# Inverse square roots of the norms: a power of -0.5 on GpSimd and one Newton step in place of a bit trick and three steps

## The chip, the cores and the metric

The kernel runs on one core of a Trainium2 chip. The metric is the device time of one execution in microseconds (us). Durations of single instructions come from one profiled execution, which has its own time and its own span (the time from the first to the last recorded instruction).

## The reference, cut to what matters

A diffusion backbone of four layers works on 256 context tokens and 256 latent tokens of width 1024. Layers 0 and 3 mix tokens by windowed attention (16 query heads, 4 key heads), layer 1 by multi-head latent attention (16 heads), layer 2 by a recurrent unit. After each mixer comes a gated feed-forward part of width 2816 with a short convolution. Every sublayer starts with a norm over the token's 1024 features, and the attentions norm every head of queries and keys, and in layer 1 also the two low-rank vectors:

```python
def rmsnorm(x, gain):
    xf = x.astype(jnp.float32)
    y = xf * lax.rsqrt(jnp.mean(xf * xf, axis=-1, keepdims=True) + EPS)
    return (y * gain.astype(jnp.float32)).astype(x.dtype)
```

## The kernel before, in words

The residual stream X lies transposed: eight tiles of 128 features by 512 tokens, context tokens in columns 0 to 255 and latent tokens in columns 256 to 511. Matrix products are made nearly exact by splitting each operand into a rounded part (hi) and the remainder (lo) and adding three products (`mm3`, lines 227 to 229: hi with hi, lo with hi, hi with lo; which operand's part is which depends on the caller). Weights come from memory in units of up to 128 x 1024 (`load`, L207), with three buffers; `convert` rounds a unit on ScalarE (whi, L214) and subtracts on GpSimd (wlo, L218), in four pieces of 256 columns or in one. This subtraction, and some of the lo parts of the normed activations (L442), are nearly all that GpSimd does.

The place of the change is `mean_rsqrt` (L276). It takes sums of squares, one column of 128 tokens (or one head) each, scales them by 1/dim and adds EPS (rs_v, L278), and returns the inverse square root. `rsqrt` (L264) halves the number's bits and subtracts them from a constant (L268, L269), and refines this guess by three Newton steps of three instructions (L271, L272, L273). All are on VectorE, each needs the one before, and each works on 128 partitions by 2, 4, 8 or 16 columns.

The callers are these. `Norm.rsq` (2 columns): squares on ScalarE and sums on VectorE (L413, L415), TensorE adds over features (L423), mean_rsqrt, and TensorE spreads the result over 128 rows (L427); `Norm.apply` then multiplies (hn, L437) and splits into h_hi (L438) and h_lo (L442 on GpSimd, L444 on VectorE). It is called once for context and once for latent tokens between any two sublayers. `out_tail` computes the context columns of a sublayer's output first, so that the context half's norm runs while TensorE does the latent columns (their result goes to X on VectorE, L452), and then calls the latent half's norm; the next sublayer's first matmuls on context columns can run beside that one. At the end of the last layer's mixer there are latent tokens only. In windowed attention, `swa` calls mean_rsqrt once for all keys (16 columns, rk; keys are scaled at L599, turned, copied at L604 and transposed on TensorE at L609), and `q_post` once for every 128 tokens and half of the heads (8 columns; the result only scales the scores later, through rqs, L640). In latent attention, `mla` calls it for the two low-rank vectors (4 columns, L789), for the keys and the queries of the first four heads (16 columns each), and then for each 128 tokens of the next four heads, keys and queries together (8 columns; kn at L832 and L833, transposed at L837, rqs at L869). The cores of the attentions score, take the exponential, transpose the probabilities (L694 or L908) and multiply by the values (L700 or L914).

The order on each engine is made when the kernel is compiled: a scheduler simulates the engines with its own costs and, each time an engine is free, takes from the ready instructions the one that comes first in the program text. So independent instructions are put between those of a call where the simulated engine would wait. On the chip every engine then runs its list in that order, and an instruction that waits holds up those behind it. In a few places the text forces an order (`tc.issue_after`), none of them in mean_rsqrt. The tiles of mean_rsqrt come from a pool of 24 small buffers.

Of the kernel before, what the change touches and what calls it, by code (L numbers as in the profile page):

```python
# [10 lines left out]
F32 = mybir.dt.float32  # L11
# [4 lines left out]
ALU = mybir.AluOpType  # L16
# [95 lines left out]
def hybrid_kernel(ctx: ExitStack, tc: tile.TileContext, xT, cc, ccT, W, modwa, modwb, modw, colv, rowv, tabs, band, out, depth=DEPTH, dbg=None):  # L112
    nc = tc.nc
    offs, _ = unit_offsets()

    const = ctx.enter_context(tc.tile_pool(name="const", bufs=1))
# [30 lines left out]
    def small(n, name="small", dt=F32):  # L147
        return sm_p.tile([128, 32], dt, tag="small", name=name)[:, :n]
# [115 lines left out]
    def rsqrt(v, n, steps=3):  # L264
        i = small(n, "rs_i", I32)
        y = small(n, "rs_y")
        t = small(n, "rs_t")
        nc.vector.tensor_scalar(i, v.bitcast(I32), 1, None, op0=ALU.logical_shift_right)  # L268
        nc.vector.tensor_scalar(y.bitcast(I32), i, -1.0, MAGIC, op0=ALU.mult, op1=ALU.add)  # L269
        for _ in range(steps):  # L270
            nc.vector.tensor_tensor(t, y, y, op=ALU.mult)  # L271
            nc.vector.scalar_tensor_tensor(t, t, -0.5, v, op0=ALU.mult, op1=ALU.mult)  # L272
            nc.vector.scalar_tensor_tensor(y, t, 1.5, y, op0=ALU.add, op1=ALU.mult)  # L273
        return y

    def mean_rsqrt(src, n, dim):  # L276
        v = small(n, "rs_v")
        nc.vector.tensor_scalar(v, src, 1.0 / dim, EPS, op0=ALU.mult, op1=ALU.add)  # L278
        return rsqrt(v, n)

    modc = [const.tile([128, 2, 48], F32, name=f"modc{l}") for l in range(DEPTH)]
    junk = const.tile([128, D], BF16, name="junk")
    scale_c = [const.tile([128, 2, 2, 8], F32, name=f"scale{l}") for l in range(DEPTH)]
# [105 lines left out]
    class Norm:  # L389
# [28 lines left out]
        def rsq(self, sums):  # L418
            acc, sq = sums
            ps = tp_ps()  # L420
            for b in range(2):
                for z, a in enumerate((acc, sq)):
                    nc.tensor.matmul(ps[:, b:b + 1], a[:, b * 128:(b + 1) * 128], ones, start=z == 0, stop=z == 1)  # L423
            rs = mean_rsqrt(ps[:, 0:2], 2, D)
            rb = ps[:, 256:]
            for b in range(2):
                nc.tensor.matmul(rb[:, b * 128:(b + 1) * 128], rs[:, b:b + 1].to_broadcast([128, 128]), ident, start=True, stop=True)  # L427
            return rb
# [97 lines left out]
    def swa(l, i, q0, nm, nxt, first=None):  # L526
# [57 lines left out]
        for b in range(4):  # L584
# [5 lines left out]
            nc.scalar.activation(sq, kb, AF.Square)  # L590
            nc.vector.tensor_reduce(ssk[:, b * 4:(b + 1) * 4], sq.rearrange("p (h d) -> p h d", d=64), axis=AX.X, op=ALU.add)
        rk = mean_rsqrt(ssk, 16, 64)
        kh, kl = big("k_hi"), big("k_lo")

# [19 lines left out]
        def q_post(p, b, ps):  # L614
            if rqs[p] is None:
                rqs[p] = const.tile([128, 32], F32, tag=f"rqs{p}", name="rqs")
            if (p, b // 2) not in qt:
                qt[p, b // 2] = big("q").rearrange("p (b j) n -> p b j n", b=2)
            qb = qt[p, b // 2][:, b % 2]
            sq = tmp("sq")  # L620
            nc.scalar.activation(sq, ps, AF.Square)
            ss = small(8, "ssq")
            nc.vector.tensor_reduce(ss, sq.rearrange("p (h d) -> p h d", d=64), axis=AX.X, op=ALU.add)
            qr = tmp("qr")
            rotate(qr, ps, b, 8, gq, cgq, sgq)
            for z in range(2):
                hl = tmp("qhl")
                h4 = hl.rearrange("p (h s d) -> p h s d", h=4, s=2)
                q4 = qr[:, z * 256:(z + 1) * 256].rearrange("p (h d) -> p h d", h=4)
                nc.scalar.activation(h4[:, :, 0].bitcast(F32R), q4, AF.Copy)  # L630
                nc.vector.tensor_tensor(h4[:, :, 1], q4, h4[:, :, 0], op=ALU.subtract)
                pq = tp_ps()
                for j in range(4):
                    nc.tensor.transpose(pq[:, j * 128:(j + 1) * 128], hl[:, j * 128:(j + 1) * 128], ident)
                if z == 0:
                    nc.scalar.activation(qb[:, z], pq, AF.Copy)
                else:
                    nc.vector.tensor_copy(qb[:, z], pq)
            rq = mean_rsqrt(ss, 8, 64)
            nc.vector.tensor_scalar(rqs[p][:, b * 8:(b + 1) * 8], rq, 0.125, None, op0=ALU.mult)  # L640
# [694 lines left out]
```

## Time and profile before

| | |
|---|---|
| median of three runs | 2244.1 us (2243.03 to 2250.57) |
| the profiled execution | 2239.54 us, span 2237.8 us |
| busy in the span: TensorE, VectorE, ScalarE, GpSimd | 2120.5, 1572.0, 1033.3, 1046.0 us |
| mean granted clock of TensorE | 0.985 of full speed |

The engines are named PE (TensorE's matmuls), PEld (its weight loads), DVE (VectorE), ACT (ScalarE), POOL (GpSimd) and SP (the queue that issues the loads from memory). L273 is line 273 of the kernel. A busy share is an average over the whole span, so which wait ends last is read stretch by stretch. A name such as wlo<-raw,whi says which tile is written and which are read.

### The profile page before, as it was taken

Reading aid. Unit: us, or ns where it says so; the run is one execution under the profiler, and the core shown is the slowest. Engines: PE = TensorE matmul, PEld = TensorE weight load, DVE = VectorE, ACT = ScalarE, POOL = GpSimd, SP = SyncE. Lnnn points to the kernel's source line nnn. Section 1 sums busy time; section 2 is a strip of 40 time slices with the busy share of each in tenths; the row PEclk is TensorE's granted clock in tenths of the full one; section 3 lists DMA queues with packets and bytes.
Section 4 is the critical chain, followed back from the end, with each engine's and each line's share of the span. In section 5 each row is a group of like instructions: output and inputs, shape, how many; then the busy total and the mean of one; then the engine's idle time right before and its main releaser. Section 6 shows DMA issues by size and latency. Waiting matters only on the chain.

```text
span 2237.8 us, 32872 instructions
## 1 busy us (share of the span) xinstructions
PE 2120.5 (95%) x12084; PEld 1762.9 (79%) x12084; DVE 1572.0 (70%) x3342; ACT 1033.3 (46%) x1850; POOL 1046.0 (47%) x760
## 2 busy tenths in 40 slices
PE   6989999999999999999999998899999999898999
PEld 5666788888878666888888786688888887678999
DVE  4677779777776887687879689847864456785333
ACT  4467653332346775532323366634332234675544
POOL 3231155444544113444554456664544444526887
PEclk9999999999999999999999999999999999999999
DMA  8534136554532001155556422234655552313665
GB/s 300 195 123 133 39 131 193 170 173 164 174 101 68 21 29 57 60 194 175 175 179 189 140 67 81 78 93 136 194 185 167 164 168 74 104 38 107 187 181 158
DMA packets 83888, 300.14 MB, mean 134 GB/s; under 512 B 11152, under 2 KB 12816, under 8 KB 81296
## 3 DMA queue, kind: packets, MB, share of 16 engines
q1 hardware_dynamic: 83728, 298.05, 41.4%
q8 instruction: 95, 1.56, 0.3%
q14 instruction: 65, 0.53, 0.1%
HBM read 296.97 MB, written 1.05 MB: 133 GB/s over the span
## 4 chain that ended last, share of the span: by engine, by line
PE 76%; DVE 16%; ACT 4%; DMA 2%; issue 1%; POOL 1%; SPq 0%; ACTq 0%; DVEq 0%
PE fl L228 9%; PE fl L229 8%; PE fl L227 8%; PE mm L227 7%; PE mm L229 7%; PE mm L228 7%; PE mo L228 4%; PE mo L227 4%; PE mo L229 4%; PE tp L227 3%; PE tp L229 2%; PE tp L228 2%; PE mo L700 2%; PE mm L887 2%; PE tp L694 2%
## 5 line engine op out<-in xcount | busy, mean ns | idle before, releaser
L218 POOL TENSOR_TENSOR wlo<-raw,whi 128x256 fp32r<-128x256 f32 (+3 forms) x709 | 1011.4, 1448 | 1121.6 <-ACT whi L214 1086.0
L214 ACT ACTIVATE whi<-raw 128x1024 fp32r<-128x1024 f32 (+3 forms) x367 | 382.6, 1043 | 478.0 <-PE tp L228 187.8
L376 DVE SCALAR_TENSOR_TENSOR junk<-mw,cbc 128x1024 bf16<-128x1024 f32 x256 | 457.6, 1788 | 24.3 <-DMA mw<-in_modw_dram 14.7
L227 PE MATMUL fl<-h_hi,whi 128*128 128x512 f32 (+1 forms) x832 | 296.8, 358 | 3.3 <-DVE lam L961 1.7
L228 PE MATMUL fl<-h_lo,whi 128*128 128x512 f32 (+1 forms) x832 | 297.3, 358 | 0.2 <-POOL h_lo L442 0.2
L229 PE MATMUL fl<-h_hi,wlo 128*128 128x512 f32 (+1 forms) x832 | 297.2, 358 | 0.1
L228 PE MATMUL mm<-h_lo,whi 128*128 128x512 f32 (+1 forms) x768 | 269.8, 352 | 2.3 <-DVE h_lo L444 1.5
L227 PE MATMUL mm<-h_hi,whi 128*128 128x512 f32 (+1 forms) x768 | 270.6, 352 | 1.3 <-ACT h_hi L438 1.1
L229 PE MATMUL mm<-h_hi,wlo 128*128 128x512 f32 (+1 forms) x768 | 269.3, 351 | 0.0
L1112 DVE SCALAR_TENSOR_TENSOR conv<-mm,colt,conv 128x510 f32<-128x510 f32 (+1 forms) x88 | 59.8, 679 | 191.7 <-ACT conv L1110 191.7
L1116 ACT ACTIVATE conv<-conv 128x512 f32<-128x512 f32 (+1 forms) x88 | 51.0, 580 | 288.9 <-DVE conv L1114 288.9
L227 PEld LDWEIGHTS fl<-h_hi,whi 128*128 128x128 f32 x832 | 157.7, 190 | 26.2 <-DVE xc L1006 1.9
L228 PEld LDWEIGHTS fl<-h_lo,whi 128*128 128x128 f32 x832 | 158.2, 190 | 23.0 <-POOL h_lo L442 0.6
L229 PEld LDWEIGHTS fl<-h_hi,wlo 128*128 128x128 f32 x832 | 158.1, 190 | 22.9 <-POOL wlo L218 0.5
L227 PE MATMUL mo<-g_hi,whi 128*128 128x256 f32 (+1 forms) x488 | 164.8, 338 | 9.4 <-DVE x L452 6.3
L228 PE MATMUL mo<-g_lo,whi 128*128 128x256 f32 (+1 forms) x488 | 164.0, 336 | 0.4 <-DVE g_lo L262 0.4
L228 PEld LDWEIGHTS mm<-h_lo,whi 128*128 128x128 f32 x768 | 146.4, 191 | 22.8 <-DVE h_lo L444 2.3
L227 PEld LDWEIGHTS mm<-h_hi,whi 128*128 128x128 f32 x768 | 147.0, 191 | 21.0 <-ACT h_hi L438 1.9
L229 PE MATMUL mo<-g_hi,wlo 128*128 128x256 f32 (+1 forms) x488 | 163.5, 335 | 0.0
L229 PEld LDWEIGHTS mm<-h_hi,wlo 128*128 128x128 f32 x768 | 146.3, 191 | 18.6
L452 DVE SCALAR_TENSOR_TENSOR x<-mo,modc,x 128x256 f32<-128x256 f32 x212 | 95.4, 477 | 85.9 <-PE mo L229 85.6
L227 PEld LDWEIGHTS mo<-g_hi,whi 128*128 128x128 f32 x488 | 92.4, 190 | 21.9 <-DVE x L452 6.7
(313 smaller groups left out, 4376.0 us busy)
## 6 DMA issues: line engine op xcount, KB each, us to landing
raw<-in_W_dram SPq DMA_DIRECT2D x352, 512.0 KB, 3.6
mw<-in_modw_dram SPq DMA_DIRECT2D x144, 512.0 KB, 4.2
mw<-in_modwa_dram SPq DMA_DIRECT2D x8, 1024.0 KB, 16.2
mw<-in_modwb_dram SPq DMA_DIRECT2D x16, 512.0 KB, 4.7
mw<-in_modwb_dram SPq DMA_DIRECT2D x8, 1024.0 KB, 9.2
cbc<-in_cc_dram SPq DMA_DIRECT2D x3, 1024.0 KB, 5.8
raw<-in_W_dram SPq DMA_DIRECT2D x8, 384.0 KB, 3.0
x<-in_xT_dram SPq DMA_DIRECT2D x8, 256.0 KB, 3.7
```

What stands on the lines that cost most here:

```text
L214: nc.scalar.activation(hi, raw, AF.Copy)
L218: nc.gpsimd.tensor_tensor(lo[:, cs], raw[:, cs], f32(hi[:, cs]), op=ALU.subtract)
L227: nc.tensor.matmul(ps, ah, bh, start=start and i == 0, stop=False, **kw)
L228: nc.tensor.matmul(ps, ah, bl, start=False, stop=False, **kw)
L229: op = nc.tensor.matmul(ps, al, bh, start=False, stop=stop and i == n - 1, **kw)
L376: nc.vector.scalar_tensor_tensor(junk, raw, 1.0, cbc[:, s], op0=ALU.mult, op1=ALU.mult, accum_out=modc[l][:, s, m:m + 1])
L452: nc.vector.scalar_tensor_tensor(X[m][:, half], ps[:, half], modc[l][:, s, part + m:part + m + 1], X[m][:, half], op0=ALU.mult, op1=ALU.add)
L694: nc.tensor.transpose(pp[:, c:c + 128], P[z][:, (2 * kp + kk) * 128:(2 * kp + kk + 1) * 128], ident)
L700: nc.tensor.matmul(po[r], v[0][:, kb, p * 128 + 64 * z:p * 128 + 64 * z + 64], pt[:, kp, (kk * 2 + z) * 128:(kk * 2 + z + 1) * 128], start ...
L887: nc.tensor.matmul(ps[:, c], d["q"][:96, 2 * hp + z, bc], d["k"][:96, 2 * hp + z, :nk], start=True, stop=True)
L1112: op = nc.vector.scalar_tensor_tensor(y3[:, :, 1:], g3[:, :, :255], cw[:, l, 0, f:f + 1], y3[:, :, 1:], op0=ALU.mult, op1=ALU.add)
L1116: nc.scalar.activation(y[:, t0:], y[:, t0:], AF.Silu)
```

## The change

`mean_rsqrt` no longer calls `rsqrt`. It hands v to GpSimd, which raises it element by element to the power in a constant tile mhalf (-0.5), and VectorE does one Newton step on the result. mhalf is filled once at the start.

```diff
     def mean_rsqrt(src, n, dim):
         v = small(n, "rs_v")
         nc.vector.tensor_scalar(v, src, 1.0 / dim, EPS, op0=ALU.mult, op1=ALU.add)
-        return rsqrt(v, n)
-
+        y = small(n, "rs_y")
+        t = small(n, "rs_t")
+        nc.gpsimd.tensor_tensor(y, v, mhalf[:, :n], op=ALU.pow)
+        nc.vector.tensor_tensor(t, y, y, op=ALU.mult)
+        nc.vector.scalar_tensor_tensor(t, t, -0.5, v, op0=ALU.mult, op1=ALU.mult)
+        nc.vector.scalar_tensor_tensor(y, t, 1.5, y, op0=ALU.add, op1=ALU.mult)
+        return y
+
+    mhalf = const.tile([128, 32], F32, name='mhalf')
+    nc.gpsimd.memset(mhalf, -0.5)
```

## Rows read from the trace of the kernel before

**Rows 1.** The page: busy time by engine; the chain that ended last, by engine.
```profile
PE 2120.5 (95%) x12084; PEld 1762.9 (79%) x12084; DVE 1572.0 (70%) x3342; ACT 1033.3 (46%) x1850; POOL 1046.0 (47%) x760
...
PE 76%; DVE 16%; ACT 4%; DMA 2%; issue 1%; POOL 1%; SPq 0%; ACTq 0%; DVEq 0%
```

**Rows 2.** Stretch, its length; PE, PEld, DVE, ACT, POOL busy (instructions); clock, DMA share, GB/s.
```profile
270.00:303.00 33.00, 29.94 (x233) 27.98 (x233) 26.70 (x69) 16.66 (x35) 14.75 (x20) 1.00 0.20 65
...
724.00:860.00 136.00, 123.90 (x814) 89.94 (x814) 112.14 (x412) 96.19 (x237) 22.61 (x34) 0.99 0.11 32
...
1900.00:1925.00 25.00, 20.77 (x85) 16.64 (x85) 13.79 (x30) 11.83 (x23) 17.27 (x24) 0.86 0.38 107
...
2025.00:2045.00 20.00, 13.91 (x93) 13.24 (x92) 13.89 (x37) 9.40 (x19) 13.10 (x18) 0.80 0.35 106
```

**Rows 3.** TensorE's waits: waiting line, what ended the wait, us, times, longest.
```profile
PE tp L427 <- DVE rs_y L273: 13.5, 11, 3.4
...
PE tp L609 <- ACT P L604: 6.7, 2, 4.2
...
PE tp L837 <- DVE rqs L869: 5.8, 2, 3.7
PE tp L837 <- DVE kn L833: 4.4, 2, 2.3
```

**Rows 4.** Groups by line, VectorE: busy us, mean ns of one, idle time before.
```profile
L273 DVE SCALAR_TENSOR_TENSOR rs_y<-rs_t,rs_y 128x8 f32<-128x8 f32 (+3 forms) x135 | 36.2, 268 | 2.4
L271 DVE TENSOR_TENSOR rs_t<-rs_y 128x8 f32<-128x8 f32 (+3 forms) x135 | 33.2, 247 | 2.6
L272 DVE SCALAR_TENSOR_TENSOR rs_t<-rs_t,rs_v 128x8 f32<-128x8 f32 (+3 forms) x135 | 31.5, 233 | 2.2
...
L269 DVE TENSOR_SCALAR rs_y<-rs_i 128x8 int32<-128x8 int32 (+3 forms) x45 | 14.7, 327 | 1.2
...
L268 DVE TENSOR_SCALAR rs_i<-rs_v 128x8 int32<-128x8 int32 (+3 forms) x45 | 11.5, 255 | 0.9
```

**Rows 5.** Tile rs_y: duration ns (min/median/max), first and last start, forms.
```profile
L269 DVE TENSOR_SCALAR rs_y<-rs_i x45: 153/172/736, 14.2 to 2036.3; 128x8 int32<-128x8 int32 x24, 128x2 int32<-128x2 int32 x15, 128x16 int32<-128x16 int32 x4, 128x4 int32<-128x4 int32 x2
```

**Rows 6.** Chain that ended last, two calls of mean_rsqrt: start us, us, what.
```profile
279.34 0.18 DVE rs_i L268
...
284.36 0.08 DVE rs_y L273
...
1910.97 0.19 DVE rs_i L268
...
1911.39 0.69 DVE rs_t L271
...
1916.24 0.66 DVE rs_t L272
...
1916.92 0.19 DVE rs_y L273
```

**Rows 7.** The same chain: a handover from ScalarE to GpSimd to TensorE.
```profile
300.48 0.07 issue
300.55 0.75 POOL h_lo L442
301.30 0.04 issue
```

**Rows 8.** GpSimd's groups by shape: busy us, mean ns of one, idle before.
```profile
L218 POOL TENSOR_TENSOR wlo<-raw,whi 128x1024 fp32r<-128x1024 f32 x248 | 641.8, 2589 | 532.9 <-ACT whi L214 529.3 <-PE mo L229 3.5
L218 POOL TENSOR_TENSOR wlo<-raw,whi 128x256 fp32r<-128x256 f32 x440 | 357.4, 844 | 569.2 <-ACT whi L214 538.9 <-issue 12.5 <-PE mo L700 6.3
...
L218 POOL TENSOR_TENSOR wlo<-raw,whi 128x128 fp32r<-128x128 f32 x12 | 5.3, 471 | 5.1 <-ACT whi L214 5.1
```

**Rows 9.** GpSimd in order of time, beside two calls of mean_rsqrt.
```profile
279.42 3.07 POOL L218 TENSOR_TENSOR wlo<-raw,whi 128x256 fp32r<-128x256 f32 x4 [8.40 <-ACT whi L214]
...
1911.30 5.56 POOL L218 TENSOR_TENSOR wlo<-raw,whi 128x256 fp32r<-128x256 f32 x8 [2.90 <-ACT whi L214]
```

## The prediction

> **What bounds the kernel now.** First the page's busy shares and its chain that ended last: TensorE is busy for 2120.5 of 2237.8 us and 76% of the chain is TensorE, 16% VectorE, 1% GpSimd [rows 1]. So no change to VectorE can give more than the 117 us in which TensorE stands idle, and a VectorE instruction counts only where TensorE waits behind it. Then the busy time by stretch shows where that idle time lies: at the seams between sublayers and in the attention stages. The seam at 270 to 303 us leaves TensorE idle for 33.00 - 29.94 = 3.1 us, multi-head latent attention (724 to 860) for 12.1, the first 25 us of layer 3 for 4.2, its last norm (2025 to 2045) for 6.1 [rows 2]. Last TensorE's waits: the broadcast of the inverse root (L427) waited 13.5 us in 11 places for the final Newton step L273, the longest time 3.4; key transposes L609 waited 6.7 in two places and L837 4.4 in two, both a few instructions behind an inverse root [rows 3].
>
> **What is removed.** mean_rsqrt runs 45 times: 24 calls on 8 columns, 15 on 2, 4 on 16, 2 on 4 [rows 5]. Each is L278 and then eleven dependent VectorE instructions, L268, L269 and three rounds of L271 to L273. L268, L269 and two of three rounds go, eight instructions a call. In busy time that is 11.5 + 14.7 + 2/3 x (33.2 + 31.5 + 36.2) = 93.5 us, 2.1 us a call [rows 4]. It isn't one price. L269 takes 172 ns at the median and up to 736 ns [rows 5]: in the call at 1910 us L268 takes 0.19, L269 as much, the eight steps after it 0.66 to 0.69 each, and the last one 0.19 again [rows 6]; GpSimd's wlo subtractions start at 1911.30 and last 5.56 us [rows 9]. So a step costs about 0.2 us with GpSimd quiet and 0.69 beside wlo; eight cost 1.6 or up to 5.5 us.
>
> **What is added.** One hop: VectorE hands v to GpSimd, GpSimd does the power, VectorE takes y. Handovers have rows: ScalarE to GpSimd 0.07 us, GpSimd to TensorE 0.04 [rows 7]; I take 0.1 for both. No row has a power on GpSimd. From below: its subtractions take 471 ns at 128 columns and 844 at 256 [rows 8], which is 2.9 ns a column and 0.1 us for none, so 0.1 us if a power costs no more than a subtraction. From above nothing bounds a routine of another kind; the longest GpSimd instruction on record is 2.59 us [rows 8], and I keep that as the upper end of what rows show. I take 0.5 us, the subtraction at 128 columns, the narrowest on record, though it has eight or more times the elements. So the hop is 0.6 us. GpSimd's queue is in order: where wlo pieces are running (0.77 each at 279.42: 3.07 for four [rows 9]) the power waits for about half of one, so 1.0. Behind it in that queue are the next weight unit's wlo pieces, which start up to 0.5 us later; their matmuls come some microseconds afterwards at the seams, so I price that at nothing, and at 0.5 us a seam if that cover is gone. VectorE's three remaining steps wait for the power, and anything that the scheduler put behind them waits too. The memset of mhalf falls into the first 2 us and costs nothing (GpSimd is idle there until the weights come); the DMA queues gain and lose nothing.
>
> **What each place gives**, in the profiled execution's own 2239.5 us (span 2237.8):
> (a) Seams after sublayers, five alike (279/293 us, and at 652, 916, 1291, 1875). The length of a call is read from the chain of waits, from the start of L268 to the end of the last L273 (the two ends of one stand in rows 6, the others are read alike). The context call at 279 takes 5.1 us, 279.34 to 284.44 [rows 6], 1.5 of it other VectorE work put between. After: 1.0 hop, 2.0 for three steps (the wlo pieces that slowed the removed steps now meet these), about 1 between: 4.0, so 1.1 less. The latent call at 293, 4.0 us, becomes 0.6 + 1.0 + 0.8 = 2.4, so 1.6 less. Together 2.7 us of VectorE path against 3.1 of TensorE idle [rows 2], part of which has other causes (PSUM taken by L452): half comes through, 1.5 each, 7.5.
> (b) The pair at 1505 and the lone call at 2035, where TensorE waits up to 3.4 us with nothing to cover it [rows 3]. 6.1 us becomes 4.0, 3.1 becomes 2.0: 3.1 together.
> (c) The three 16-column calls whose consumers are the key transposes (64, 704, 1910 us): 4.3, 4.2 and 6.1 us (1910.97 to 1917.11 [rows 6]) become 1.0 + 2.0 = 3.0: 1.3, 1.2, 3.1, within TensorE's waits there (6.7 for the two L609, 2.3 the longest for L837 [rows 3]): 5.6.
> (d) The 12 query calls in window attention and the 13 others in latent attention. 1.6 removed, 0.6 to 1.0 added: 0.6 to 1.0 of VectorE time each, some 20 us over 25 calls, but most stand beside core work. TensorE waits 10.2 us for L837 in four places [rows 3], and about a third of that is such a call: 4, and 2 for window attention: 6.
> (e) The two calls before 17 us: nothing, since TensorE there waits next for weights from memory.
> Sum 22.2. I take 2 off for powers that delay VectorE's other instructions behind them: 20 us, 2239.5 to 2219.5. The median of the runs shown, 2244.1, lies 4.6 above the profiled execution, so on that scale 2224. What I count at nothing: the mean granted clock is 0.86 and 0.80 in two of these stretches [rows 2], between the levels of 1.2 and 2.4 GHz, where TensorE had waited up to 4.2 and 3.4 us [rows 3]. If shorter waits kept it at 2.4 GHz, up to 25 x 0.14 + 20 x 0.20 = 7.5 us more come back. That is the low end.
>
> **A rule weighed.** A VectorE step beside wlo takes 0.66 to 0.69 us instead of 0.19 [rows 6], about one wlo piece. The Trainium skill, SBUF — State Buffer, section Who interferes with whom, says that an instruction with two SBUF inputs on VectorE and a GpSimd instruction that reads SBUF exclude each other for the whole instruction; the rows agree. By it VectorE is not free during the power: other two-input work beside it waits it out, which at 0.5 us in 25 calls, half on the path, takes 6 us off the 20.
>
> **Rivals.**
> R1, forecast: the power costs at most about 1 us: 2224.
> R2, slower: the power is dear. Place: the 8- and 16-column calls of the two attentions, whose keys and score scales wait for it. Point: a hop dearer than the 2.25 us that eight steps with their gaps take on average, so a power of about 2.1 us. At 2.6 (rows' upper end) a hop is 2.7: the seams and lone calls keep some 2 us, the 13 latent calls lose 1.1 each on the path, 14, the others 2: 2258. Each further microsecond falls on the some 25 calls that are on the chain, two thirds of them uncovered: 17 us. For it: a power is no single arithmetic step. Against: only 2 to 16 columns.
> R3, no difference: the power is cheap but stands in GpSimd's queue behind whole weight units (3.07 to 5.56 us [rows 9]) whose whi the chip finishes later than the compile-time order assumed, so y comes as late as now; the 8.40 us for which wlo waited for whi at 279 show that a late one ahead is possible [rows 9]. The gain is then only the freed VectorE time: 2240.
> R4: exclusion decides: the three steps kept and the interleaved work meet wlo and the power at 0.69 us a piece, and only places (b) and (c) pay, 8.7 us: 2235.
>
> **How the numbers follow.** R1 0.50, R4 0.10, R3 0.15, R2 0.25. Below 2205 (twice the sum, or all 22 us with the clock's 7.5 and hops of 0.3) I leave 0.08, above 2265 (a power of about 3 us) 0.12. About 0.3%, 6.7 us, is what can be told from no change: faster 0.60, same 0.15, slower 0.25. R1's own range is 2210 to 2234.
>
> **What would show it.** L268 and L269 gone, 45 of each of L271 to L273 left; VectorE's busy time down by about 90 us; a GpSimd line of 45 powers whose mean is the one number that decides: under 1 us for R1, over 2 for R2. The wait of L427 for L273 should fall from 13.5 to about 7 us, those of L609 from 6.7 to 3. R3 shows as powers that wait behind wlo in GpSimd's queue. I am wrong if VectorE is seen waiting for GpSimd more than 25 us in all, or if the seams keep their 3.1 us of idle TensorE.

## The result and the profile after

The kernel after takes 2293.5 us (median of four runs, 2291.2 to 2294.6) against 2243.6 before: ratio 1.0224, 95% interval 1.0204 to 1.0244. It is 50 us slower; 20 us faster was forecast. Its profiled execution took 2292.9 us with a span of 2290.8. Lines from 281 on are eight higher than before (L427 is now L435, L609 L617, L837 L845).

The page of the kernel after, busy time by engine:
```profile
PE 2136.9 (93%) x12084; PEld 1774.2 (77%) x12084; DVE 1506.9 (66%) x2982; ACT 1033.6 (45%) x1850; POOL 1109.0 (48%) x806
```
VectorE has 360 instructions less, as planned, and is busy 65 us less, not the 90 us expected [rows 1]. The first kept step now often meets a wlo piece: L282 has a median of 674 ns in this trace, L283 and L284 of 163 and 164. TensorE's busy time rose by 16 us with the same number of instructions.

GpSimd's groups by shape after, the powers only (busy us, mean ns of one, idle before):
```profile
L281 POOL TENSOR_TENSOR rs_y<-rs_v,mhalf 128x8 f32<-128x8 f32 x24 | 40.1, 1672 | 172.9 <-DVE rs_v L278 172.9
...
L281 POOL TENSOR_TENSOR rs_y<-rs_v,mhalf 128x16 f32<-128x16 f32 x4 | 11.6, 2900 | 12.6 <-DVE rs_v L278 12.6
L281 POOL TENSOR_TENSOR rs_y<-rs_v,mhalf 128x2 f32<-128x2 f32 x15 | 10.5, 697 | 66.9 <-DVE rs_v L278 66.3 <-DVE rs_t L283 0.5
...
L281 POOL TENSOR_TENSOR rs_y<-rs_v,mhalf 128x4 f32<-128x4 f32 x2 | 2.0, 1008 | 1.0 <-DVE rs_v L278 0.9
```
A power goes by its columns: (2900 - 697) / 14 = 157 ns a column and about 0.38 us besides. The mean is 1.43 us, not 0.5.

The waits after, of TensorE, VectorE and GpSimd (who, for what; us in total, times, longest):
```profile
POOL rs_y L281 <- DVE rs_v L278: 252.7, 32, 14.4
...
DVE rs_t L282 <- POOL rs_y L281: 70.3, 43, 3.7
...
PE tp L845 <- DVE rqs L877: 18.1, 7, 3.5
...
PE tp L435 <- DVE rs_y L284: 15.2, 11, 2.8
...
PE tp L617 <- ACT P L612: 10.5, 2, 5.6
...
PE mm L228 <- POOL h_lo L450: 5.6, 3, 2.3
...
PE tp L845 <- DVE kn L841: 4.9, 1, 4.9
```
VectorE stands for 70.3 us in 43 of the 45 calls. TensorE's wait for the norms' root went up, from 13.5 to 15.2, where 7 was expected; that for the keys in latent attention from 10.2 to 23.0, and for layer 0's and 3's keys from 6.7 to 10.5 [rows 3].

Busy time by stretch after; the stretches are the shifted ones of before [rows 2], columns as there:
```profile
282.60:315.60 33.00, 28.67 (x222) 27.80 (x221) 23.50 (x54) 16.92 (x36) 16.21 (x22) 0.95 0.19 65
742.00:905.00 163.00, 135.49 (x806) 94.66 (x807) 96.41 (x317) 97.01 (x238) 40.42 (x44) 0.92 0.08 25
1949.00:1974.00 25.00, 19.43 (x80) 15.42 (x79) 10.64 (x20) 11.36 (x21) 18.37 (x23) 0.86 0.37 106
2079.00:2099.00 20.00, 14.45 (x96) 13.78 (x95) 12.27 (x30) 9.85 (x20) 13.98 (x19) 0.76 0.35 106
```
Latent attention takes 163 us instead of 136: TensorE's idle time grew from 12.1 to 27.5 us, and its busy time by 11.6 for the same work, as the mean granted clock fell from 0.99 to 0.92 of 2.4 GHz (part of the stretch at 1.2 GHz) with the longer waits. Counting from one norm's v to the next, the stretch between layer 1's two norms (664 to 916 us before) holds 32.6 of the 53 us between the two profiled executions, layer 0's attention 11, layer 3's 6; the recurrent layer's gains 5. From a seam's context v to its latent v four seams take 1.0 to 1.6 us longer (one takes 2.2 less, one 0.5 less), though their calls became shorter: at the first one 5.3 to 3.0 us and 4.2 to 2.3.

In latent attention too the call is shorter, 4.6 us on average before and 3.9 after over the 12 repeated calls. What changed is what VectorE does in it. VectorE in order of time, one call before:
```profile
788.93 0.17 DVE L271 TENSOR_TENSOR rs_t<-rs_y 128x8 f32<-128x8 f32 x1
789.01 0.68 DVE L894 TENSOR_REDUCE st<-mm 128x2 f32<-128x512 f32 x1
...
790.07 0.16 DVE L272 SCALAR_TENSOR_TENSOR rs_t<-rs_t,rs_v 128x8 f32<-128x8 f32 x1
790.14 0.15 DVE L895 TENSOR_TENSOR st<-st,rqs 128x2 f32<-128x2 f32 x1
790.21 0.68 DVE L891 TENSOR_REDUCE st<-mm 128x1 f32<-128x512 f32 x1
790.81 0.16 DVE L273 SCALAR_TENSOR_TENSOR rs_y<-rs_t,rs_y 128x8 f32<-128x8 f32 x1
```
And one call after, VectorE first, then GpSimd:
```profile
842.23 0.28 DVE L278 TENSOR_SCALAR rs_v<-ss 128x8 f32<-128x8 f32 x1
842.42 0.28 DVE L866 TENSOR_TENSOR qn<-qn,sq 128x128 f32<-128x128 f32 x1
846.45 0.41 DVE L282 TENSOR_TENSOR rs_t<-rs_y 128x8 f32<-128x8 f32 x1 [3.74 <-POOL rs_y L281]
```
```profile
841.75 3.07 POOL L218 TENSOR_TENSOR wlo<-raw,whi 128x256 fp32r<-128x256 f32 x5 [3.46 <-ACT whi L214]
844.78 1.63 POOL L281 TENSOR_TENSOR rs_y<-rs_v,mhalf 128x8 f32<-128x8 f32 x1
```
Before, the attention core's maxima (L891, L894) ran between the Newton steps, 2.2 us of other work in a mean call. After, VectorE's list has the Newton step almost at once behind v, with 0.9 us of other work in a mean call. In this call VectorE stands for 3.74 us, of which 2.1 are the power waiting behind wlo and 1.6 its own length. It is the longest of the 12: in nine of them the power starts 0.08 us behind v, and VectorE stands for 1.3 to 1.8 us, about the power's own length. Of all 45 powers 11 start later than that, 15 us together, ten of them behind wlo or h_lo pieces.

### The profile page after: what moved, and what is told of

It is laid out like the page before. It is cut to its first block, busy times and chain, and to the rows that moved or that the text cites. A ratio compares the mean times of both kernels' runs of the same rounds, so it can differ in the third digit from the quotient of the medians.

```text
span 2290.8 us, 32559 instructions
## 1 busy us (share of the span) xinstructions
PE 2136.9 (93%) x12084; PEld 1774.2 (77%) x12084; DVE 1506.9 (66%) x2982; ACT 1033.6 (45%) x1850; POOL 1109.0 (48%) x806
## 4 chain that ended last, share of the span: by engine, by line
PE 46%; DVE 7%; POOL 3%; issue 3%; ACT 1%; DMA 1%; SPq 0%; POOLq 0%; ACTq 0%
PE fl L227 5%; PE fl L229 5%; PE fl L228 5%; PE mm L227 4%; PE mm L228 4%; PE mm L229 4%; PE mo L227 3%; PE mo L228 3%; POOL wlo L218 3%; PE mo L229 3%; PE tp L227 2%; PE tp L229 2%; PE tp L228 2%; DVE junk L384 1%; PE mo L708 1%
## 5 line engine op out<-in xcount | busy, mean ns | idle before, releaser
L1120 DVE SCALAR_TENSOR_TENSOR conv<-mm,colt,conv 128x510 f32<-128x510 f32 (+1 forms) x88 | 59.8, 679 | 196.6 <-ACT conv L1118 196.6
L281 POOL TENSOR_TENSOR rs_y<-rs_v,mhalf 128x8 f32<-128x8 f32 (+3 forms) x45 | 64.2, 1427 | 253.4 <-DVE rs_v L278 252.7
```

Source lines behind the costliest of these rows:

```text
L281: nc.gpsimd.tensor_tensor(y, v, mhalf[:, :n], op=ALU.pow)
L1120: op = nc.vector.scalar_tensor_tensor(y3[:, :, 1:], g3[:, :, :255], cw[:, l, 0, f:f + 1], y3[:, :, 1:], op0=ALU.mult, op1=ALU.add)
```

## Experiments

Theories: **price** (the power's own length is paid by VectorE standing still, and TensorE behind it); **queue** (GpSimd's in-order list: wlo behind powers that wait for v, 252.7 us in all); **order** (the new order on all engines). All ratios are to the kernel before on the same chip, with 95% intervals.

**Price against the rest.**
```diff
-        nc.gpsimd.tensor_tensor(y, v, mhalf[:, :n], op=ALU.pow)
+        nc.gpsimd.tensor_tensor(y, v, mhalf[:, :n], op=ALU.mult)
...
-    nc.gpsimd.memset(mhalf, -0.5)
+    nc.gpsimd.memset(mhalf, 0.02)
```


> The kernel after, with the power replaced by a multiplication on GpSimd of the same tiles (the norms come out wrong: the roots are not computed). Every engine's list of instructions is the same as in the kernel after, so only the length of the 45 GpSimd instructions differs: 64 us in all after, some 7 us expected (0.1 to 0.2 each). If the power's own length is what costs (theory price), the time falls from 2293 to 2240 or below. If it is the in-order queue of GpSimd and the new order of instructions (theory queue and order), the time stays above 2270, about 15 us of powers having come off the path.

2242.0 us, 1.0009 (0.9993 to 1.0024): the whole loss is gone. GpSimd's widest and narrowest group, and VectorE's wait for it, in this kernel:
```profile
L281 POOL TENSOR_TENSOR rs_y<-rs_v,mhalf 128x2 f32<-128x2 f32 x15 | 2.9, 193 | 67.7 <-DVE rs_v L278 66.6 <-DVE rs_t L283 1.0
L281 POOL TENSOR_TENSOR rs_y<-rs_v,mhalf 128x16 f32<-128x16 f32 x4 | 0.9, 218 | 13.0 <-DVE rs_v L278 13.0
```
```profile
DVE rs_t L282 <- POOL rs_y L281: 19.4, 35, 2.3
```
A multiplication takes about 0.2 us whatever its width. With identical lists on every engine, 54 us less of GpSimd took 50.9 us from VectorE's wait (70.3 to 19.4) and 48 us from the time (0.0215 x 2242). GpSimd still waits as long for v (251.5 us), so neither that queue nor the order costs the 50 us. The same run says that a hop with an operation of 0.2 us, in place of eight VectorE steps, gains nothing (VectorE still waits 19.4 us): the forecast's 20 us were not there even at a smaller price than assumed.

**Removal without a hop.**
```diff
-        return rsqrt(v, n)
+        return rsqrt(v, n, 1)
```


> The kernel before with one Newton step in place of three, nothing on GpSimd (the roots are less exact: two steps are left out). 270 VectorE instructions less and no hop. The prediction's own arithmetic gives 6/8 of what removal is worth without the hop's 0.6 to 1.0 us a call: about 25 us less, 2218. If shorter calls make the compile-time order worse at the seams, as in the kernel after, where the calls at the seams are 2 us shorter and the seams 1 us longer, the gain is under 8 us.

2229.7 us, 0.9947 (0.9926 to 0.9967): 12 us, half of the 25 and above the 8. Against the multiplication (1.0009) it is 14 us less, with two more VectorE instructions a call and no wait for GpSimd: about what removal brings, even a cheap hop takes away. The two kernels have different orders, so this split is not exact. From v to v, the stretch with latent attention gains 5.0 us, the recurrent layer's 4.8, the one up to layer 3's last norm 2.8; three seams lose 1.1 to 1.7 us each and layer 0's feed-forward part 3.0.

**GpSimd's queue alone**, nobody waiting for the result:
```diff
+        d = small(n, "rs_d")
+        nc.gpsimd.tensor_tensor(d, v, mhalf[:, :n], op=ALU.mult)
         return rsqrt(v, n)
```


> The kernel before, all three steps kept, with a multiplication of v by a constant on GpSimd added in every call, whose result nobody reads. GpSimd's queue stops at each until v is there, as in the kernel after, and nothing waits for the result. Queue: 15 us or more slower than before (2260), since wlo pieces behind it start later. Price: 2244 to 2248.

2240.8 us, 1.0000 (0.9984 to 1.0016). The second kernel has ALU.pow in that line:

> As the one with the multiplication whose result nobody reads, with a power in its place; the lists of all engines are the same as there. The difference of the two is what 57 us more of busy GpSimd costs where nobody waits for the result. Price on the path: within 3 us of the multiplication. Queue: 5 to 15 us slower than the multiplication.

2244.3 us, 0.9997 (0.9982 to 1.0011). GpSimd waited over 210 us for v in both, and 64 us of powers ran: no loss. Queue falls as a cause; GpSimd has room. Nor does a power hold VectorE: in this kernel 109 Newton steps ran wholly inside a power and took 147 to 178 ns each, as with GpSimd quiet. VectorE and GpSimd in one call:
```profile
705.00 0.17 DVE L271 TENSOR_TENSOR rs_t<-rs_y 128x16 f32<-128x16 f32 x1
705.21 0.17 DVE L272 SCALAR_TENSOR_TENSOR rs_t<-rs_t,rs_v 128x16 f32<-128x16 f32 x1
705.42 0.17 DVE L273 SCALAR_TENSOR_TENSOR rs_y<-rs_t,rs_y 128x16 f32<-128x16 f32 x1
```
```profile
704.63 2.90 POOL L280 TENSOR_TENSOR rs_d<-rs_v,mhalf 128x16 f32<-128x16 f32 x1 [5.05 <-DVE rs_v L278]
```

**By place.** Power and one step in the norms alone, in latent attention alone, in window attention alone (mean_bit is the old mean_rsqrt, mean_pow the new one; the two other kernels likewise):
```diff
-            rs = mean_bit(ps[:, 0:2], 2, D)
+            rs = mean_pow(ps[:, 0:2], 2, D)
```


> Power and one step only in the 15 calls of the norms (2 columns, 0.70 us each); the attentions keep bit trick and three steps. Price: a hop of 0.8 us against 8 steps that took 1.6 us or more, so nothing lost: 2235 to 2245. Order: the seams in the kernel after lost 1 to 2 us each over before although the calls were 2 us shorter; if that comes from the new order of instructions it comes again here: 2248 to 2255.

2244.5 us, 1.0018 (1.0006 to 1.0030).

> Power and one step only in the 16 calls of latent attention (12 of 8 columns at 1.64 us, 2 of 16 at 2.90, 2 of 4 at 1.01). This layer's mixer lost some 29 to 32 us of the 50 between before and after. Price: 2270 to 2276, with TensorE's mean granted clock in that stretch near 0.91 again.

2275.6 us, 1.0154 (1.0137 to 1.0170), VectorE waiting 32.4 us; the clock from 710 to 890 us was 0.92.

> Power and one step only in the 14 calls of window attention (12 of 8 columns, 2 of 16). Layers 0 and 3 lost some 12 us together in the kernel after. Price: 2250 to 2256. With the norms' and latent attention's runs the three losses should add up to 50 within 8 us.

2257.0 us, 1.0071 (1.0055 to 1.0088), a microsecond above the expected range, VectorE waiting 23.5 us. The three add up to 1.0243, the whole change to 1.0224. Nearly all of the loss lies in the attentions, whose calls are 4, 8 and 16 columns wide.

**More of the price.**
```diff
+        nc.gpsimd.tensor_tensor(small(n, "rs_d"), v, mhalf[:, :n], op=ALU.pow)
         nc.gpsimd.tensor_tensor(y, v, mhalf[:, :n], op=ALU.pow)
```


> The kernel after, with each power done twice on GpSimd, the first into a tile that nobody reads: the hop is longer by one power (1.64 us at 8 columns, 0.7 at 2, 2.9 at 16). If the time goes by the power's length on the path, 64 us more on GpSimd cost again 45 to 65 us: 2340 to 2358. If most of the loss were one-off (a new order, one handover), under 2310.

2368.1 us (two runs), 1.0577 (1.0558 to 1.0596), 75 us above the kernel after by the medians and 79 by the ratios, more than either expectation. VectorE's wait in this kernel:
```profile
DVE rs_t L283 <- POOL rs_y L282: 130.1, 45, 6.5
```
The wait grew by 60 us and the time by 75; the mean granted clock was 0.955 here and 0.975 after. So here each further microsecond of a power cost about one and more.

**Covering the power.** In latent attention the Newton step and its users move behind the next core:
```diff
+                flush()
                 core(hg, h // 2, 2 + h % 2)
...
-                    rr = mean_rsqrt(ss, 8, 96)
-                    kv_put(hg + 1, b, kb, rr[:, 0:4])
-                    q_scale(hg + 1, b, 1, rr[:, 4:8])
+                    flush()
+                    late.append((hg + 1, b, kb, *rsqrt_begin(ss, 8, 96)))
```
(rsqrt_begin makes v and issues the power; flush does the Newton step, kv_put and q_scale of all that is in late.)

> The kernel after, with the Newton step of the 12 repeated calls in latent attention, and what uses its result, written one attention core later in the text, so that VectorE has a core's instructions to run while GpSimd computes the power. The power keeps its length. If the loss there is VectorE standing in its in-order queue before the power's result (the compile-time order took the power for a short instruction), half or more of latent attention's 30 us comes back: 2262 to 2278. If the key transposes wait for the power itself whatever VectorE does meanwhile, it stays at 2288 to 2296.

2279.1 us, 1.0171 (1.0150 to 1.0192), just above the first expectation: 0.0053, some 12 us, came back, somewhat under half of latent attention's 33. VectorE's wait for GpSimd fell from 70.3 to 59.8 us. From the first repeated call's v to the last one's the stretch took 5.5 us more than before, against 22.1 in the kernel after. Its control:

> The control of the deferred kernel: bit trick and three steps on VectorE everywhere (nothing on GpSimd), but in the 12 repeated calls of latent attention these steps and what uses them are written one core later, as there. If the later place is good by itself, this is faster than before, 2232 to 2238; if the 14 us that it gave the power came from covering the power, this stays at 2240 to 2248.

2243.6 us, 1.0017 (1.0004 to 1.0031), so the later place gives nothing by itself: it covered part of the power.

> Power and one step only in the 12 repeated calls of latent attention, in their later place; all other calls as in the kernel before. If the later place covers the power, what was left of latent attention's loss in the deferred kernel (19 of 33 us) belongs to the two 16-column and two 4-column calls at its start, and this takes 2240 to 2248. If these 12 calls still cost, 2252 to 2262.

2251.0 us, 1.0053 (1.0039 to 1.0066), just under the second expectation: in their later place the 12 calls still cost 12 us, and VectorE still waits 12.8 us for them (23.4 in the kernel after), so they are covered by half. By difference, the 16-column and 4-column calls at the start of latent attention cost some of what remains of the 33; that was not run by itself.

**Why the seams' gain did not come.** GpSimd in order of time at the seam of 279 us before (the unit ahead stands in [rows 9]), then in the kernel with one step and no hop, then after:
```profile
284.38 3.00 POOL L218 TENSOR_TENSOR wlo<-raw,whi 128x256 fp32r<-128x256 f32 x4 [1.89 <-ACT whi L214]
288.33 3.38 POOL L218 TENSOR_TENSOR wlo<-raw,whi 128x256 fp32r<-128x256 f32 x4 [0.95 <-ACT whi L214]
291.67 0.90 POOL L442 TENSOR_TENSOR h_lo<-hw,h_hi 128x256 fp32r<-128x256 f32 x1
```
```profile
285.52 6.52 POOL L218 TENSOR_TENSOR wlo<-raw,whi 128x256 fp32r<-128x256 f32 x8 [2.96 <-ACT whi L214]
292.01 2.45 POOL L442 TENSOR_TENSOR h_lo<-hw,h_hi 128x256 fp32r<-128x256 f32 x3
```
```profile
298.00 6.58 POOL L218 TENSOR_TENSOR wlo<-raw,whi 128x256 fp32r<-128x256 f32 x8 [2.37 <-ACT whi L214]
304.54 1.41 POOL L450 TENSOR_TENSOR h_lo<-hw,h_hi 128x256 fp32r<-128x256 f32 x2
```
Where the call is shorter, the activations come earlier and the weight rounding later in ScalarE's list; two units' subtractions then run in one block of eight, and h_lo stands behind it. Test: h_lo of the context half off GpSimd, once with the power in the norms, once with the bit trick.
```diff
-                if j in ((4, 5, 6, 7) if s else (2, 5)):
+                if j in (() if s else (2, 5)):
```


> Power only in the norms, as in the run that lost 2 us there, and the context half's h_lo tiles 4 to 7 made on VectorE instead of GpSimd. If the seams gain nothing from their shorter calls because TensorE then waits for h_lo that stands behind eight wlo pieces in GpSimd's queue (5.6 + 2.3 + 1.3 us of such waits in that run), these waits go and the time falls 5 us or more more than in the control: ratio to before 0.3% or more lower than the control's. If the seam's loss lies elsewhere, it stays within 2 us of the control.

2237.7 us, 0.9979 (0.9963 to 0.9994).

> The control: the kernel before with the context half's h_lo tiles 4 to 7 on VectorE instead of GpSimd, bit trick and three steps kept. More work on VectorE at the seams, where it is busy: 2243 to 2252 by either theory.

2255.7 us, 1.0054 (1.0035 to 1.0073), above what either theory expected. TensorE's waits for h_lo, first with the power in the norms and h_lo on GpSimd, then with it on VectorE:
```profile
PE mm L228 <- POOL h_lo L455: 5.6, 3, 2.3
...
PE fl L228 <- POOL h_lo L455: 2.3, 1, 2.3
PE mm L229 <- POOL h_lo L455: 1.3, 2, 1.1
```
```profile
PE mm L228 <- DVE h_lo L457: 0.5, 2, 0.3
```
9.2 us of waits became 0.5, and the time fell by 0.0039, 8.7 us, against the norms' kernel. With the long calls the same edit loses 12 us; why is not known. From context v to latent v at the first seam, before, with the power in the norms, and with h_lo on VectorE too (columns as in [rows 2]):
```profile
279.10:293.10 14.00, 11.63 (x89) 10.61 (x89) 12.54 (x30) 7.57 (x16) 10.31 (x13) 1.00 0.25 82
```
```profile
282.80:298.70 15.90, 11.58 (x84) 10.97 (x83) 11.53 (x23) 8.40 (x18) 11.64 (x15) 0.91 0.29 100
```
```profile
284.10:300.20 16.10, 13.67 (x105) 12.69 (x105) 13.79 (x29) 7.54 (x16) 10.11 (x13) 1.00 0.28 99
```
TensorE stands idle there for 2.4, 4.3 (2.3 of it one wait for h_lo) and 2.4 us. So h_lo behind wlo cost what this seam lost, and without it the seam is as idle as before, and not less. That the shorter calls gain anything at the seams is therefore not shown, and as every edit gives a new order, the 8.7 us are not all shown to be these waits. This kernel, power in the norms alone and h_lo on VectorE, is 0.2% under the one before, by an interval that just leaves out no change.

**Fewer steps, no GpSimd.** Two Newton steps everywhere (`return rsqrt(v, n, 2)`):

> The kernel before with two Newton steps in place of three and no GpSimd (about five correct digits in the root instead of seven): 135 VectorE instructions less. One step gave 12 us for 270 instructions, so half: 2236, ratio 0.997. A candidate that beats both kernels.

2237.6 us, 0.9993 (0.9983 to 1.0003). And two steps in the attentions alone:

> No GpSimd power: two Newton steps in the attentions' 30 calls, three in the norms' 15. One step everywhere gave 7 us in the attentions and lost 1 to 3 us at most seams. So the seams should stay as before and the attentions give about 4 us: 2236 to 2238, ratio 0.997 to 0.999.

2240.3 us, 0.9996 (0.9979 to 1.0013). Both fall short of what was expected, and neither differs from before by more than the measurement can tell.

## Why the prediction was wrong

- **The power's price, the step that failed first.** "I take 0.5 us, the subtraction at 128 columns, the narrowest on record": it took 0.70, 1.01, 1.67 and 2.90 us at 2, 4, 8 and 16 columns, 1.43 on average. The subtractions' slope (2.9 ns a column) said nothing about an operation of another kind, whose slope is 157 ns a column. The handover was right: v's end to the power's start is 0.08 us and the power's end to L282 0.03 in most calls.
- **The exchange rate, the step that failed second.** "1.6 removed, 0.6 to 1.0 added" set a microsecond of VectorE steps against a microsecond of hop. They aren't worth the same. The steps had other instructions between them, so six a call removed gave 12 us over 45 calls, 0.27 us a call. A wait for GpSimd is an empty place in VectorE's in-order list, and 50.9 us of it were worth 48. R2's point, a power of 2.1 us, was therefore far too high: 0.2 us only breaks even. This step is the larger miss: with the measured 1.67 us in it, place (d) has a latent call lose 0.2 us (1.6 removed, 1.8 added), where latent attention's 16 calls lost 33, 2.1 a call.
- **R2 was the case that came**, by its place (the 8- and 16-column calls of the attentions: 33 and 15 of 50 us) and its mechanism, at a price under its own point and with an effect above its 2258. Its 17 us for each further microsecond were a third of what was measured: doubled powers, 1.41 us more a call, cost 75 us, 53 a microsecond.
- **R3** is refuted as a cause of the 50 us: powers waited behind wlo in a few calls, up to 2.8 us, but the multiplication in the same lists lost nothing. With that cheap operation, though, the time is the one that R3 gives, no difference (2242.0); how much of the missing gain is the waiting behind wlo was not separated.
- **R4** and the weighed rule: VectorE's kept steps do meet wlo at 0.67 us, as the Trainium skill's SBUF — State Buffer page, Who interferes with whom, says of the shared port pair, and this is 16 us of the 28 by which the fall of VectorE's busy time, 65 us, stays under the 93.5 (the kept steps take 49.7 us, a third of the old rounds 33.6). It is no part of the 50: the multiplication has nearly the same meetings (45.4 us). What the prediction drew from the rule, that VectorE is not free during the power, did not come: two-input steps inside a power took 147 to 178 ns. There the rule and the measurement differ, and the measurement decides.
- **Place (a)** was right that the calls get shorter (5.3 to 3.0 us, 4.2 to 2.3, by more than it took off) and wrong in "half comes through": nothing did, and h_lo then stood behind wlo. Half of its 2.7 is 1.35 and not 1.5, and the two 4-column calls stand in no place of the sum.
- **The clock**, counted at nothing with a possible gain, was a loss: 0.99 to 0.92 in latent attention, where TensorE's busy time grew by 11.6 us.
- **Its signs**: VectorE waited 70.3 us for GpSimd, where 25 was to show it wrong, and the seam at 279 us kept its idle TensorE, 4.3 us (33.00 - 28.67) after 3.1. The mean power, 1.43 us, lay between its two marks of 1 and 2 and did not decide.

## What to carry to other kernels

An operation that no row shows has no price, and a row of another operation on the same engine doesn't give one: measure it alone before it goes on a dependent chain, at each width. Moving steps of a chain to another engine exchanges work that the compile-time order had filled with other instructions for a wait that it has not filled; ask what VectorE's list holds between the issue and the use, and if nothing, write the use later in the text. When a call at a seam gets shorter, look at what moves ahead and what then stands behind it in the other engines' lists.

## What the runs showed of the hardware that was not expected

On GpSimd a power of two fp32 tiles costs 157 ns a column above 0.38 us, a multiplication 0.19 to 0.24 us from 2 to 16 columns. 64 us of powers that nobody waits for cost nothing measurable (0.9997), though GpSimd then waits 210 us for VectorE's v. A two-input VectorE step of 128 x 2 to 16 takes 0.65 us at the median beside a wlo subtraction and 0.17 inside a power.
